# One fp32 layer on one core: weight-sum additions and additions of squares given to GpSimd, other buffers for the low halves of W_O's last product, six low halves no longer stored

## The chip, the cores and the metric

The kernel runs on 1 core of one Trainium2 chip. The metric is the device time of one execution in microseconds. The engines are TensorE (PE in the profile; its weight loads are PEld), VectorE (DVE), ScalarE (ACT), GpSimd (POOL) and SyncE (SP, which here only issues DMAs). GpSimd issues DMAs too, on a queue of its own.

## The reference, cut

One layer over 2112 tokens (2048 of a prompt, 64 of a sample with a state of its own), model width 1024, everything in fp32:

```
h      = rms_norm(x, g_pre);   proj = h @ w_in        # ten projections of 1024 columns
vA, bA, cA, zA, q, f, iv, zB, gA, gB = split(proj)
yA     = (silu(zA) * bA * causal_conv3(cA * vA)) @ w_a_out                  # path A
fg     = lb + (1 - lb) * sigmoid(f)
o      = hgrn2_scan(S0, silu(q) * scale, 1 - fg, iv, log(fg))  # path B: 8 heads, state 128 x 128, chunks of 64
yB     = (rms_norm(o) * silu(zB)) @ w_b_out
out    = (sigmoid(gA) * yA + sigmoid(gB) * yB) @ w_o
x      = x + rms_norm(out, g_post)
gate   = sigmoid(rms_norm(x, g_ple) @ w_ple_gate);    x = x + (p @ w_ple_proj) * gate
```

Results are the new x of both streams, the last columns of the convolution and the states of path B.

## The kernel before

**Numbers.** Activations lie with features on the 128 partitions and tokens along the columns. TensorE multiplies at a rounded form of fp32, so each operand is split into a high half (a cast, ScalarE) and a low half (the operand minus its high half, VectorE, `split`, L196). A product is three matmuls for each slice of 128 features: high x high, high x low, low x high (L380 to L382 in `sgroup`, L514 to L516 in `in_turn`). The third one reads the low half of the weights.

**Tokens.** They are worked through in three blocks of 768, 704 and 640 columns. Each is handled as two halves of 384, 352 and 320 columns.

**Seven products in place of eight.** Weights are taken in pairs of column blocks, which gives 2 x 2 quarters (A11, A12, A21, A22) against two halves of the features and two halves of the tokens. A pair takes seven products, with sums of weight quarters (S1 to S4) and sums of activations (T1 to T4). `sgroup` does the seven products of one pair one after another; the input projections go so. Its first group after W_O (by_k) begins with four products side by side, so it needs the low halves of S3, S1 and S2 at about the same time. `in_turn` does product 1 for four pairs, then product 2 for four pairs, and so on, over the stages W_A, W_B and W_O: 3 x 7 x 4 steps of 12 matmuls. Product 3 uses S2, product 4 S3, product 6 S1, product 7 S4. After each of products 2, 5, 6 and 7 in W_O, the stage's `sink` puts a finished piece of the output into xo (L427 where it is an addition), and `sum_squares` squares it on ScalarE (L635) and adds the square to an accumulator on VectorE (L636). `final_norm` reads that accumulator in the next block's first groups: transposes on TensorE (L616), a reduction on VectorE (L617), a reciprocal root on GpSimd (L576), and then one load of x per row block (L1185, GpSimd's queue).

**Where weight sums come from.** In the first block, the sums for the input projections are made in `combined`. Those for W_A, W_B and W_O are made in `prepare_sums`, 12 pairs of four sums, while path B (7 pairs) and path A (5 pairs) run: GpSimd's queue loads the four quarters (L338), VectorE adds (L361), GpSimd's queue stores the sum (L343), ScalarE and VectorE split it, and GpSimd's queue stores the low half (L347). Later passages, 6 pairs with 24 additions, do the same for groups used in the last block. After that a sum is loaded by SP's queue (`raw<-S`, L206), cast by ScalarE, and its low half is loaded by SP's queue too (L228).

**Buffers for low halves.** A loaded low half gets one of 4 `lo` buffers or one of 3 `s` buffers, by a counter:

```
def low_tile():
    turn[0] += 1
    return sum_tile(F32R) if turn[0] % 7 in (1, 3, 5) else lo_tile()
```

Buffers of a kind are used in rotation, and SP's queue works in order: a load into a buffer whose last reader hasn't finished holds what is queued behind it. Low halves that are made for the first time go into `lo` and are stored for later blocks (L234, SP's queue) if `split_w` was given a key.

**Order.** Engines take their instructions in an order that a list scheduler sets when the kernel is built, with marks in the code that tie side work to places in the stream of matmuls (`hooks`, `behind_all`, `issue_after`). `plain_group` does a pair without sums, with eight products, where the sums are not there yet: it opens the first block.

Of the kernel before, what the change touches and what calls it, by code (L numbers as in the profile page):

```python
# [14 lines left out]
ALU = mybir.AluOpType  # L15
# [17 lines left out]
W_A, W_B, W_O, W_G = 80, 88, 96, 104  # L33
# [55 lines left out]
def hybrid_step(  # L89
# [41 lines left out]
    def wide(x):  # L131
        return x.shape[1]
# [71 lines left out]
    def load_raw(src):  # L204
        raw = wp.tile([P, 4, P], F32, tag="raw", name=nm("raw"), bufs=5)
        SP.dma_start(raw, src)  # L206
        return raw
# [118 lines left out]
    def pairs_of(idx):  # L326
        return [(idx + g, idx + KH + g) for g in range(KH)]

    def prepare_sums(groups):


        def tile_of(dt=F32):
            return rt(4 * P, dt).rearrange("p (k c) -> p k c", c=P)

        def load(i1, i2):
            out = [tile_of() for _ in range(4)]
            for t, (i, h) in zip(out, ((i1, 0), (i2, 0), (i2, 1), (i1, 1))):
                G.dma_start(t, w_blk[i, h])  # L338
            return out

        def keep(name, i1, s):
            sums.setdefault(i1, {})[name] = dram.tile([P, 4, P], F32, tag=f"{name}_{i1}", name=nm(name), bufs=1)
            G.dma_start(sums[i1][name], s)  # L343
            lows[i1, name] = dram.tile([P, 4, P], F32, tag=f"lo{i1, name}", name=nm("low"), bufs=1)
            lo = tile_of(F32R)
            split(s, lo, lo)
            G.dma_start(lows[i1, name], lo.bitcast(F32))  # L347

        nxt = load(*groups[0])
        yield  # L350
        for n, (i1, i2) in enumerate(groups):
            a11, a21, a22, a12 = nxt
            if n + 1 < len(groups):
                nxt = load(*groups[n + 1])
            for name, out, x, y, op in (
                ("S1", a22, a21, a22, ALU.add),
                ("S3", a21, a11, a21, ALU.subtract),
                ("S2", a11, a22, a11, ALU.subtract),
                ("S4", a12, a12, a11, ALU.subtract),
            ):  # L360
                V.tensor_tensor(out, x, y, op)  # L361
                keep(name, i1, out)
                yield

# [46 lines left out]
    def half(t, h):  # L411
        n = wide(t) // 2
        return t[:, h * n : (h + 1) * n]
# [15 lines left out]
    def plain_group(i1, i2, hs, sink, raws=None, between=None):  # L429


        w, ps = {}, {}

        def split_of(c, h):
            key = ((i1, i2)[c], h)
            raw = raws[c, h] if raws else load_raw(w_blk[key])
            with nullcontext() if raws else tc.high_priority():
                w[c, h] = split_w(raw, None if (c, h) == (1, 0) else key)

        for c, h in ((0, 0), (1, 0)) if between else ((0, 0), (0, 1), (1, 0), (1, 1)):  # L440
            with behind_all(() if between else summed[2 + c]):
                split_of(c, h)

        def add(c, ks):
            for k in ks:
                hi, lo = w[c, k // KH]
                for h in range(2):
                    xhi, xlo = hs[k][h]
                    if (c, h) not in ps:
                        ps[c, h] = ps_gemm(wide(xhi))  # L450
                    T.matmul(ps[c, h], hi[:, k % KH, :], xhi, start=k == 0, stop=False)
                    T.matmul(ps[c, h], hi[:, k % KH, :], xlo, start=False, stop=False)
                    last[0] = T.matmul(ps[c, h], lo[:, k % KH, :], xhi, start=False, stop=k == KB - 1).ins

        if between:
            for k in range(KB):
                between()
                for c in range(2):
                    if k == 2:
                        split_of(c, 1)  # L460
                    with placed():
                        add(c, (k,))
        for c in range(2):
            if not between:
                with placed():
                    add(c, range(KB))
            for h in range(2):
                sink(c, h, ps[c, h], None)
# [19 lines left out]
    def in_turn(stages, operand):  # L488


        todo = [(st, n) for st in stages for n in range(7)]
        made = {0: operand}

        def prepare(i, k):
            if i < len(todo):
                st, n = todo[i]
                made.setdefault(i, []).append(operand_of(st["raw"], IN_TURN[n][1], k))

        for i, (st, n) in enumerate(todo):
            if n == 0:  # L500
                st["mid"], st["bank"] = [], {}
            xs = made.pop(i)
            for g in range(KH):
                i1, i2 = st["idx"] + g, st["idx"] + KH + g
                with tc.high_priority():
                    hi, lo = kept_w(i1, i2, IN_TURN[n][0], IN_TURN[n][0] in st["anew"])
                start = n in (0, 2, 3, 5)
                if start:
                    st["bank"][g] = ps_gemm(wide(xs[0][0]))
                ps = st["bank"][g]  # L510
                add = partial(T.matmul, ps, skip_group_check=not start)
                for k in range(KH):
                    xhi, xlo = xs[k]
                    add(hi[:, k, :], xhi, start=start and k == 0, stop=False)  # L514
                    add(hi[:, k, :], xlo, start=False, stop=False)  # L515
                    last[0] = add(lo[:, k, :], xhi, start=False, stop=k == KH - 1).ins  # L516
                if n == 6:
                    prepare(i + 1, g)
                if n == 0:
                    st["mid"].append(rt(2 * wide(ps)))  # L520
                    with tc.high_priority():
                        copies[0] = A.copy(half(st["mid"][g], 0), ps).ins
                u2, p7 = half(st["mid"][g], 0), half(st["mid"][g], 1)
                if n == 1:
                    st["sink"](g, 0, 0, ps, None)
                elif n == 2:
                    adds[0] = V.tensor_tensor(u2, u2, ps, ALU.add).ins
                elif n == 3:
                    with tc.high_priority():
                        copies[0] = A.copy(p7, ps).ins  # L530
                elif n == 4:
                    st["sink"](g, 1, 0, u2, ps)
                elif n == 5:
                    p5 = hf(wide(ps))
                    with tc.high_priority():
                        copies[0] = A.copy(p5, ps).ins
                    adds[0] = V.tensor_tensor(p7, p7, p5, ALU.add).ins
                    st["sink"](g, 1, 1, u2, p7)
                elif n == 6:
                    st["sink"](g, 0, 1, u2, ps)  # L540
                if n < 6:
                    prepare(i + 1, g)
                hook()
                yield st["idx"], n, g
# [82 lines left out]
            copy(out[:, cols_of(sg)], spread(col, sg["n"]))  # L627
        yield

    def sum_squares(j, src, acc, n):  # L630
        if j == 0:
            A.activation(acc, src, AF.Square)
        else:
            sq = hf(n) if n <= MAXN // 2 else rt(n)
            A.activation(sq, src, AF.Square)  # L635
            V.tensor_tensor(acc, acc, sq, ALU.add)  # L636

    def load_x(bl, k):
        t = rt(bl["n"])
# [513 lines left out]
            dict(idx=W_B, raw=ob, sink=sink_b, anew=("A11", "A12")),  # L1153
        ], loads

    def out_in_turn(mg, xo, acc, anew):
        xo.extend([None] * KB)
        begun = set()

        def sink(g, c, h, x, y):  # L1160
            j = g + c * KH
            if not acc:
                acc.append(rt(wide(mg[0])))
            if xo[j] is None:
                xo[j] = rt(wide(mg[0]))
            v = half(xo[j], h)
            into(v, x, y)
            sum_squares(int(h in begun), v, half(acc[0], h), wide(v))
            begun.add(h)

        return dict(idx=W_O, raw=mg, sink=sink, anew=anew)
# [198 lines left out]
    for bi, bl in enumerate(blocks):  # L1370
# [3 lines left out]
        late = [(FF * 8, QQ * 8), (GB * 8 + KB - 2, GB * 8 + KB - 1)]  # L1374
        in_heads = (pairs_of(W_A) + pairs_of(W_B))[:-1] if first else late if middle else None
        in_path = pairs_of(W_B)[-1:] + pairs_of(W_O) if first else pairs_of(W_G) if bl["last"] else None
        extra = prepare_sums(in_heads) if in_heads else None
        path_b(bl, hc, first, kept, fills, hs if first else None, extra, (0, 2) if first else (0,))
        run(fills)
        a = []  # L1380
# [15 lines left out]
        def ready():  # L1396
            a_first.extend(narrow(half(t, 0)) for t in a[:KH])

        path_a(bl, hc, a, first, side(rows, prepare_sums(in_path) if in_path else None), ready)
        assert not hooks and (extra is None or next(extra, extra) is extra)  # L1400
        mg, xo, h2, acc = [], [], [], []
        stages, loads = merge_in_turn(a, kept, mg)
        stages.append(out_in_turn(mg, xo, acc, ("A11", "A12", "A22") if bl["last"] else ()))
        if nxt:
            hc = new_operands()
            ops = operands_in_steps(hc, cols, partial(load_x, nxt), nxt["n"])
# [88 lines left out]
```

## Time and profile before

| | |
|---|---|
| time, median of 3 runs | 2575.61 us (2574.92 to 2575.83) |
| the profiled execution | 2570.03 us, span 2567.7 us, mean granted TensorE clock 0.999 |
| TensorE busy | 2543.4 us, 99% of the span, 16246 matmuls |
| VectorE busy | 1886.0 us, 73% |
| ScalarE busy | 1591.9 us, 62% |
| GpSimd busy | 391.0 us, 15% |
| SP's queue, share of 16 DMA engines | 59.5% (510.59 MB) |
| GpSimd's queue, share of 16 DMA engines | 18.0% (166.25 MB) |

The span is the time from the first to the last recorded instruction of the profiled execution. Busy time is the time in which an engine has at least one instruction at work, without DMA issues. A row of the trace such as `880.17 0.34 PE L516 MATMUL pg<-r,s ...` is one or more instructions: start and length in us, engine, line, operation, output tile `<-` input tiles, shape. What stands in square brackets behind it is how long the engine had been idle before and what ended that wait. `pg` is an accumulator of TensorE in PSUM, `r` a buffer of activations or of `prepare_sums`, `hf` a half-width one, `hi`, `lo` and `s` are the buffers of weights. SPq is SP's DMA queue.

### The profile page before, as it was taken

What the parts mean: (1) busy time and instruction counts of PE and PEld (TensorE: products, weight loads), DVE (VectorE), ACT (ScalarE), POOL (GpSimd) and SP (SyncE); (2) the same over time, 40 slices, a digit from 0 to 9 for tenths busy, and PEclk for the clock granted to TensorE, in tenths of its full rate; (3) what the DMA queues carried; (4) which work ended last, traced back from release to release, by engine and by line L of the source; (5) the groups of instructions that cost most, each with busy time, mean ns of one, the idle gap of its engine ahead of it and who ended that gap; (6) DMA issues with size and microseconds to landing.
All of it is one profiled execution on the core that took longest, in us unless ns stands there. A gap on an engine that the chain in (4) does not pass through costs nothing. (4 is left out here: it accounts for less than half of the span.)

```text
span 2567.7 us, 47073 instructions
## 1 busy us (share of the span) xinstructions
PE 2543.4 (99%) x16246; PEld 2528.9 (98%) x16246; DVE 1886.0 (73%) x3630; ACT 1591.9 (62%) x3076; POOL 391.0 (15%) x718
## 2 busy tenths in 40 slices
PE   8999999999999999999999999999999999999999
PEld 8999999999999999999999999999999999999998
DVE  8788888899989865666665557986566666678966
ACT  6666676554555664577774545676677765566736
POOL 1022121222110021121011101102100011111221
PEclk9999999999999999999999999999999999999999
DMA  7678777898798797676557768989866678899977
GB/s 274 211 262 276 275 251 262 296 318 305 265 324 269 249 341 271 202 241 199 183 180 237 232 212 303 318 279 336 312 199 194 201 240 291 302 309 344 308 263 259
DMA packets 324847, 679.89 MB, mean 265 GB/s; under 512 B 40544, under 2 KB 45184, under 8 KB 324608
## 3 DMA queue, kind: packets, MB, share of 16 engines
q1 hardware_dynamic: 281664, 510.59, 59.5%
q0 software_dynamic: 42656, 166.25, 18.0%
q8 instruction: 128, 2.10, 0.3%
q14 instruction: 111, 0.91, 0.1%
q10 hardware_dynamic: 288, 0.05, 0.0%
HBM read 496.61 MB, written 180.11 MB: 264 GB/s over the span
## 5 line engine op out<-in xcount | busy, mean ns | idle before, releaser
L380 PE MATMUL pg<-r,hi 128*128 128x320 f32 (+2 forms) x3304 | 1088.6, 329 | 0.0
L381 PE MATMUL pg<-r,hi 128*128 128x320 f32 (+2 forms) x3304 | 1067.7, 323 | 0.0
L382 PE MATMUL pg<-r,lo 128*128 128x384 f32 (+2 forms) x2368 | 772.0, 326 | 1.2 <-DMA lo<-low 1.2
L381 PEld LDWEIGHTS pg<-r,hi 128*128 128x128 f32 x3304 | 623.3, 189 | 0.0
L380 PEld LDWEIGHTS pg<-r,hi 128*128 128x128 f32 x3304 | 622.6, 188 | 0.4
L227 ACT CAST hi<-raw 128x512 fp32r<-128x512 f32 x528 | 325.7, 619 | 337.7 <-PE pg L381 154.1
L196 ACT CAST hi<-raw 128x512 fp32r<-128x512 f32 x458 | 283.4, 620 | 309.4 <-PE pg L381 137.9
L382 PEld LDWEIGHTS pg<-r,lo 128*128 128x128 f32 x2368 | 445.4, 188 | 1.6 <-DMA lo<-low 1.4
L196 DVE TENSOR_TENSOR lo<-raw,hi 128x512 fp32r<-128x512 f32 x458 | 315.4, 690 | 168.2 <-ACT hi L196 127.2
L515 PE MATMUL pg<-r,hi 128*128 128x320 f32 (+2 forms) x1120 | 360.8, 324 | 1.1 <-DVE r L196 0.8
L514 PE MATMUL pg<-r,hi 128*128 128x320 f32 (+2 forms) x1120 | 354.5, 324 | 1.1 <-ACT r L196 1.1
L382 PE MATMUL pg<-r,s 128*128 128x320 f32 (+1 forms) x936 | 296.6, 317 | 3.4 <-DMA s<-low 3.4
L196 DVE TENSOR_TENSOR r<-r,r 128x320 fp32r<-128x320 f32 (+7 forms) x394 | 230.8, 604 | 63.7 <-ACT r L196 62.3
L516 PE MATMUL pg<-r,lo 128*128 128x320 f32 (+2 forms) x776 | 249.8, 323 | 5.0 <-DMA lo<-low 5.0
L196 ACT CAST r<-r 128x320 fp32r<-128x320 f32 (+7 forms) x394 | 205.9, 552 | 16.7 <-DVE r L361 5.6
L515 PEld LDWEIGHTS pg<-r,hi 128*128 128x128 f32 x1120 | 210.6, 188 | 5.0 <-DVE r L196 4.2
L514 PEld LDWEIGHTS pg<-r,hi 128*128 128x128 f32 x1120 | 208.4, 188 | 4.9 <-ACT r L196 4.5
L382 PEld LDWEIGHTS pg<-r,s 128*128 128x128 f32 x936 | 176.8, 189 | 4.0 <-DMA s<-low 4.0
L196 ACT CAST hi<-s 128x512 fp32r<-128x512 f32 x160 | 98.7, 618 | 118.8 <-PE pg L381 103.4
L394 ACT COPY hf<-pg 128x352 f32<-128x352 f32 (+2 forms) x354 | 155.9, 443 | 8.9 <-PE pg L382 8.7
L516 PEld LDWEIGHTS pg<-r,lo 128*128 128x128 f32 x776 | 145.8, 188 | 6.3 <-DMA lo<-low 6.2
L196 DVE TENSOR_TENSOR lo<-s,hi 128x512 fp32r<-128x512 f32 x160 | 110.3, 689 | 36.7 <-PE pg L382 12.8
(367 smaller groups left out, 3846.7 us busy)
## 6 DMA issues: line engine op xcount, KB each, us to landing
raw<-w_blk SPq DMA_DIRECT2D x554, 256.0 KB, 3.9
raw<-S SPq DMA_DIRECT2D x472, 256.0 KB, 3.7
s<-low SPq DMA_DIRECT2D x327, 256.0 KB, 3.9
lo<-low SPq DMA_DIRECT2D x201, 256.0 KB, 4.3
low<-lo SPq DMA_DIRECT2D x194, 256.0 KB, 3.0
S<-s SPq DMA_DIRECT2D x152, 256.0 KB, 3.1
r<-w_blk POOLq DMA_DIRECT2D x72, 256.0 KB, 6.5
S<-r POOLq DMA_DIRECT2D x72, 256.0 KB, 3.4
```

Source lines behind the costliest of these rows:

```text
L196: return A.copy(hi, src).ins, V.tensor_tensor(lo, src, hi.bitcast(F32), ALU.subtract).ins
L227: A.copy(hi, raw)
L380: add(hi[:, k, :], xhi, start=start and k == 0, stop=False)
L381: add(hi[:, k, :], xlo, start=False, stop=False)
L382: last[0] = add(lo[:, k, :], xhi, start=False, stop=k == KH - 1).ins
L394: copied = A.copy(got[n], ps[bank])
L514: add(hi[:, k, :], xhi, start=start and k == 0, stop=False)
L515: add(hi[:, k, :], xlo, start=False, stop=False)
L516: last[0] = add(lo[:, k, :], xhi, start=False, stop=k == KH - 1).ins
```

## The change

1. `prepare_sums` takes the engine of its additions as an argument: GpSimd in the first block (48 additions of 128 x 512), VectorE in the two later passages (24).
2. `sum_squares` takes the engine of its addition: GpSimd for W_O of the first two blocks (14 additions of 128 x 384, 14 of 128 x 352), VectorE everywhere else.
3. Ahead of product 7 of W_O, in each block, the counter of `low_tile` is set to 3. The four low halves of that product then go into `lo, s, lo, lo`.
4. `plain_group` no longer gives `split_w` a key: six low halves fewer are stored by SP's queue in the first block.

```diff
-    def prepare_sums(groups):
+    def prepare_sums(groups, E):
...
-                V.tensor_tensor(out, x, y, op)
+                E.tensor_tensor(out, x, y, op)
                 keep(name, i1, out)
...
         def split_of(c, h):
-            key = ((i1, i2)[c], h)
-            raw = raws[c, h] if raws else load_raw(w_blk[key])
+            raw = raws[c, h] if raws else load_raw(w_blk[(i1, i2)[c], h])
             with nullcontext() if raws else tc.high_priority():
-                w[c, h] = split_w(raw, None if (c, h) == (1, 0) else key)
+                w[c, h] = split_w(raw)
...
             xs = made.pop(i)
+            if (st["idx"], n) == (W_O, 6):
+                turn[0] = 3
...
-    def sum_squares(j, src, acc, n):
+    def sum_squares(j, src, acc, n, E=V):
...
-            V.tensor_tensor(acc, acc, sq, ALU.add)
+            E.tensor_tensor(acc, acc, sq, ALU.add)
...
-    def out_in_turn(mg, xo, acc, anew):
+    def out_in_turn(mg, xo, acc, anew, E):
...
-            sum_squares(int(h in begun), v, half(acc[0], h), wide(v))
+            sum_squares(int(h in begun), v, half(acc[0], h), wide(v), E)
...
-        extra = prepare_sums(in_heads) if in_heads else None
+        extra = prepare_sums(in_heads, G if first else V) if in_heads else None
...
-        path_a(bl, hc, a, first, side(rows, prepare_sums(in_path) if in_path else None), ready)
+        path_a(bl, hc, a, first, side(rows, prepare_sums(in_path, G if first else V) if in_path else None), ready)
...
-        stages.append(out_in_turn(mg, xo, acc, ("A11", "A12", "A22") if bl["last"] else ()))
+        stages.append(out_in_turn(mg, xo, acc, ("A11", "A12", "A22") if bl["last"] else (), V if bl["last"] else G))
```

Two places of the order that the scheduler now sets. The first is SP's queue at the end of W_O in the first block. `raw<-S` loads a full sum, `s<-low` a stored low half into an `s` buffer, `low<-lo` stores a low half; loads into `lo` stand on lines of their own elsewhere. Before, the first row belongs to product 6, pair 3, the next two `s` rows to product 7, pairs 1 and 3:

```order
L228 DMA s_10952<-low_7887 128x512
L206 DMA raw_10920<-S_1882_7452 128x512
L234 DMA low_10783<-lo_10780 128x512
L228 DMA s_11010<-low_7272 128x512
L206 DMA raw_10949<-S_1981_7885 128x512
L234 DMA low_10811<-lo_10808 128x512
L206 DMA raw_10978<-S_2113_8378 128x512
L234 DMA low_10839<-lo_10836 128x512
L206 DMA raw_11007<-S_1833_7270 128x512
L206 DMA raw_11030<-S_1972_7812 128x512
L228 DMA s_11056<-low_8247 128x512
```

After:

```order
L228 DMA s_10940<-low_7875 128x512
L206 DMA raw_10908<-S_1876_7440 128x512
L234 DMA low_10771<-lo_10768 128x512
L228 DMA s_11021<-low_7802 128x512
L206 DMA raw_10937<-S_1975_7873 128x512
L234 DMA low_10799<-lo_10796 128x512
L206 DMA raw_10966<-S_2107_8366 128x512
L234 DMA low_10827<-lo_10824 128x512
L206 DMA raw_10995<-S_1827_7258 128x512
L234 DMA low_10855<-lo_10852 128x512
L206 DMA raw_11018<-S_1966_7800 128x512
L228 DMA s_11117<-low_1591 128x512
```

Now the second `s` row is product 7, pair 2, and the last one is already the next block's first gates (S3): of product 7 only one low half is in an `s` buffer.

The second place is GpSimd's queue at the end of W_O in the first block. The loads of `x_fm` at L640 (L641 after) are the next block's x, those at L1185 (L1186) the norm's x. Before:

```order
L640 DMA r_10281<-x_fm 128x704
L640 DMA r_10283<-x_fm 128x704
L640 DMA r_10916<-x_fm 128x704
L640 DMA r_10918<-x_fm 128x704
L1185 DMA r_11221<-x_fm 128x768
L1185 DMA r_11223<-x_fm 128x768
L1185 DMA r_11225<-x_fm 128x768
L1185 DMA r_11227<-x_fm 128x768
L576 TENSOR_TENSOR colsum_11229<-colsum_11229,mhalf 128x6
```

After:

```order
L637 TENSOR_TENSOR r_10449<-r_10449,hf_10843 128x384
L641 DMA r_10904<-x_fm 128x704
L637 TENSOR_TENSOR r_10449<-r_10449,hf_10871 128x384
L641 DMA r_10906<-x_fm 128x704
L637 TENSOR_TENSOR r_10449<-r_10449,hf_10931 128x384
L637 TENSOR_TENSOR r_10449<-r_10449,hf_10960 128x384
L637 TENSOR_TENSOR r_10449<-r_10449,hf_10989 128x384
L637 TENSOR_TENSOR r_10449<-r_10449,hf_11014 128x384
L637 TENSOR_TENSOR r_10449<-r_10449,hf_11037 128x384
L637 TENSOR_TENSOR r_10449<-r_10449,hf_11060 128x384
L637 TENSOR_TENSOR r_10449<-r_10449,hf_11089 128x384
L1186 DMA r_11209<-x_fm 128x768
```

Nine additions of squares now stand ahead of the norm's first load of x, two of them ahead of or between the last two loads of the next block's x.

## The prediction

> **What bounds the kernel now.** I read the page's engine lines first, then TensorE's waits, then the timeline around the longest of them. The page's line gives share and count of busy time:
>
> ```profile
> PE 2543.4 (99%) x16246; PEld 2528.9 (98%) x16246; DVE 1886.0 (73%) x3630; ACT 1591.9 (62%) x3076; POOL 391.0 (15%) x718
> ```
>
> TensorE is busy all but 24.3 of 2567.7 us, and the change leaves its matmuls as they are. So it can only win back waits, or add some. These are all of TensorE's waits (total, number, longest):
>
> ```profile
> PE pa L1095 <- ACT r L196: 6.9, 1, 6.9
> PE pg L516 <- DMA lo<-low: 5.0, 4, 2.5
> PE pg L382 <- DMA s<-low: 3.4, 2, 2.2
> PE pg L382 <- DMA lo<-low: 1.2, 1, 1.2
> PE pg L514 <- ACT r L196: 1.1, 1, 1.1
> PE pg L515 <- DVE r L196: 0.8, 2, 0.7
> ```
>
> The 6.9 is the start, before any work has arrived. Of the other 11.5 us, 9.6 are low halves that come late by DMA, 1.1 ScalarE's, 0.8 VectorE's. Only two waits stand where the change moves a buffer: the 3.4 on `s<-low`, one at each passage from W_O to the next block's first gates. The first of them (SP's lines are DMA issues; start, length):
>
> ```profile
> 880.17 0.34 PE L516 MATMUL pg<-r,s 128*128 128x384 f32 x1
> ...
> 884.04 0.33 PE L381 MATMUL pg<-r,hi 128*128 128x352 f32 x1
> 886.53 0.43 PE L382 MATMUL pg<-r,s 128*128 128x352 f32 x1 [2.16 <-DMA s<-low]
> ```
> ```profile
> 876.35 0.33 SPq L228 DMA_DIRECT2D s<-low  x1
> 877.10 0.33 SPq L206 DMA_DIRECT2D raw<-S  x1
> 879.31 0.33 SPq L206 DMA_DIRECT2D raw<-w_blk  x1
> 880.53 0.34 SPq L228 DMA_DIRECT2D s<-low  x1
> ```
>
> The load at 880.53 starts as the last matmul that reads an `s` buffer ends (880.17 + 0.34 = 880.51): W_O's product 7, pair 3. It fills the freed buffer with S2's low half for the first gates, due at 884.04 + 0.16 = 884.20, and it lands 6.0 us after its issue. And for a while after this wait TensorE runs slowly (third number from the right is the granted clock):
>
> ```profile
> 887.40:890.90 3.50, 3.50 (x15) 3.50 (x14) 0.78 (x1) 0.00 (x0) 0.00 (x0) 0.52 0.28 109
> 891.20:894.70 3.50, 3.50 (x26) 3.47 (x25) 0.99 (x2) 1.93 (x5) 0.00 (x0) 1.00 0.12 14
> ```
>
> At clock 0.52 these 3.5 us lose 3.5 x 0.48 = 1.7. The second passage has the same wait without a slow stretch:
>
> ```profile
> 1725.66 0.32 SPq L228 DMA_DIRECT2D s<-low  x1
> ...
> 1730.46 0.42 PE L382 MATMUL pg<-r,s 128*128 128x320 f32 x1 [1.27 <-DMA s<-low]
> ```
>
> **The change, part by part.**
>
> *Buffers of W_O's last products.* With the counter at 3, product 7 takes `lo, s, lo, lo` where both first blocks had `s, lo, s, lo`. The last reader of an `s` buffer is pair 2, one pair earlier. A pair is 12 matmuls. A window without a wait (each column here and above: busy time and count of TensorE, its weight loads, VectorE, ScalarE, GpSimd, then clock, DMA share, GB/s) gives their rate:
>
> ```profile
> 513.50:577.70 64.20, 64.20 (x368) 64.20 (x367) 60.29 (x108) 37.98 (x83) 18.24 (x33) 1.00 0.91 318
> ```
>
> 64.2 / 368 = 0.174 us at 384 columns, so 2.1 a pair; at 352 columns 0.160, so 1.9. The third `s` load can go at 880.53 - 2.1 = 878.4, since of the transfers ahead of it on SP's queue only the sum's raw tile (877.10) remains; the raw tile of 879.31 now stands behind it. It lands at 886.5 - 2.1 = 884.4: 0.2 late instead of 2.16 (about 2.3 against an unbroken stream). Gain 2.1; between 0, if another wait on SP's queue holds it, and 2.3. In the second passage it lands 1.9 earlier and the whole 1.27 goes; between 0 and 1.4. The third `lo` of product 7 reuses a buffer of product 6, pair 2, free some 8 us before its use: nothing. The slow stretch I take to follow from the wait, with no other gap of TensorE near it: gain 1.7; between 0 and 1.7.
>
> [...]
>
> *Weight sums on GpSimd.* 48 of the 72 adds at L361 leave VectorE, and 28 of the 70 at L636. Their rows, and the nearest ones on POOL:
>
> ```profile
> L361 DVE TENSOR_TENSOR r<-r,r 128x512 f32<-128x512 f32 x72 | 49.4, 687 | 0.2
> L636 DVE TENSOR_TENSOR r<-r,hf 128x384 f32<-128x384 f32 x14 | 7.8, 559 | 1.4 <-ACT hf L635 1.3
> L636 DVE TENSOR_TENSOR r<-r,hf 128x352 f32<-128x352 f32 x14 | 7.3, 523 | 0.6 <-ACT hf L635 0.6
> L870 POOL MEMSET hf<- 128x64 f32 x8 | 1.4, 170 | 0.0
> ```
>
> VectorE sheds 48 x 0.69 + 14 x 0.56 + 14 x 0.52 = 48 us. No row has an add on POOL. Below, it is bounded by VectorE's 0.69 for 512 columns; above by the memset, 170 / 64 = 2.7 ns a column for one stream, 1.36 us for 512, 4.1 for an add's three streams. I take 1.4, twice VectorE's row, because the operation and shape are that row's; 1.1 at 384, 1.0 at 352. POOL gains 48 x 1.4 + 14 x 1.1 + 14 x 1.0 = 97 us (48 to 250) on 391 busy: it stays idle most of the time. On its queue the add now comes ahead of the store of the same sum (L343), where it waited for VectorE anyway, so that the store is not later; the squareroot steps (L576) stand behind the same stores of low halves as before. Sums are read first in W_A, far later. In all that time, 64 to 702 us, TensorE waits for nothing, so the relief is worth nothing; and the cover for a mishap is VectorE's idle time, least in the window of 513.50 above and the two behind it (VectorE is the third pair):
>
> ```profile
> 577.70:641.90 64.20, 64.20 (x368) 64.20 (x367) 59.11 (x100) 30.79 (x58) 15.14 (x29) 1.00 0.88 305
> 641.90:706.10 64.20, 64.20 (x370) 64.16 (x369) 58.50 (x99) 33.81 (x65) 10.30 (x20) 1.00 0.80 265
> ```
>
> 14.7 us idle in 192.6; the 19 adds there take 13 us out of VectorE's load. Cost 0.
>
> *Squares in W_O.* The 28 adds at L636 sit in W_O of blocks 1 and 2, one per pair of products 2, 5, 6 and 7. Behind them on POOL's queue now stand loads of the next block's x (L640) and of the norm's x (L1185):
>
> ```profile
> 864.91 1.07 POOL L640 DMA_DIRECT2D r<-x_fm  x2 [57.96 <-PE pg L516]
> 878.50 0.54 POOL L1185 DMA_DIRECT2D r<-x_fm  x1 [12.52 <-DVE r L427]
> ```
>
> The second L640 goes after the add of product 5, pair 4, some 3 us later; VectorE takes up that tile at 878.1, 9 us after. L1185 goes behind the last add, at 887, and is added first after the norm's scale, past 898. The sum of squares itself ends about as before:
>
> ```profile
> 886.03 0.55 DVE L636 TENSOR_TENSOR r<-r,hf 128x384 f32<-128x384 f32 x1
> 886.50 1.69 DVE L196 TENSOR_TENSOR r<-r,r 128x704 fp32r<-128x704 f32 x2
> 894.14 0.82 PE L616 MATMUL pa<-ident,r 128*128 128x128 f32 x6
> ```
>
> The gates start at 882.4 (880.17 + 13 x 0.174: one pair is left). TensorE's transposes come 48 matmuls of 0.160 later, 7.7 us: at 890.1 without the wait. The last product's addition stands at 883.77, its square 0.55 + 0.5 later, an add of 1.1 ends at 886: hidden by 4 us. VectorE, without a gap from 874 to 888, drops seven of these adds, 3.3 us, so that the splits of 886.50 come earlier; TensorE does not wait for them. Gain 0, of at most the 0.8 in the list.
>
> *Fewer low halves stored.* Six stores of 256 KB in the first 60 to 100 us go from SP's queue, each 0.4 us of issue. TensorE waits for no load there. Nothing.
>
> Sum: 2.1 + 1.7 + 1.3 = 5.1 us. The profiled execution took 2570.03, its span 2567.7: 2570.03 - 5.1 = 2564.9. The median of the runs shown lies 5.6 above that execution (2575.61), and the same step gives 2570.5.
>
> **Rivals.**
>
> [...]
>
> 2. *GpSimd's adds hold VectorE up*, so that the relief turns round. At the end of W_O seven adds of 1.1 cost 7.7 against 3.3 saved; the second split of 886.50 (T2's last operand, done at 887.4) moves to 891.8, due at 882.4 + 45 x 0.160 = 889.6: TensorE waits 2. With 1 at the second passage: gain 2, 2573.5. Against it: a two-input addition of VectorE ran its usual 0.69 us wholly inside an operation of POOL that reads SBUF:
> ```profile
> 131.22 1.04 POOL L576 TENSOR_TENSOR ms<-ms,mhalf 128x4 f32<-128x4 f32 x1 [63.40 <-DVE ms L574]
> 131.50 0.69 DVE L314 TENSOR_TENSOR s<-raw,raw 128x512 f32<-128x512 f32 x1
> ```
> That one reads only four columns, though. [...]
>
> 3. *Slower: the squares come too late for the norm.* If an add takes 3.1 us (the upper bound, 4.1 x 384/512), eleven of them from 866 end at 900, 10 us behind the transposes at 890.1, and TensorE stands, here and (2.8 each, about 8) at the second passage: 18 - 5 = 13 slower, 2588. It decides from 2.2 us an add, (890.1 - 866) / 11. Against it: that takes four times VectorE's duration.
>
> 4. *The low halves of W_O and W_A land otherwise*: `s` and `lo` alternate differently from there on, and SP's order is a new one, so that the 5.0 us of waits at L516 may grow or shrink by 3 to 5: 2565 or 2575.
>
> **How the numbers follow.** 0.2% of the median, 5.15 us, is about what a measurement can tell from no change, and my sum lies on that edge. The forecast, 2570.5 (own range 2568 to 2573), has chance 0.50, half of it beyond the edge on the fast side, with some weight for the small terms that I put at 0: 0.30. Rival 1 has 0.13, of it 0.03 faster; rival 2 has 0.15, of it 0.03 slower (VectorE filling up between 513 and 706 too, from 1.4 + 0.1 us per add on: 14.7 idle + 13 saved, over 19); rival 3 has 0.07, all slower; rival 4 has 0.15, of it 0.08 faster and 0.03 slower. Faster 0.41, same 0.46, slower 0.13. The range, 2563 to 2580, leaves out rival 3 and the tails of 2 and 4.
>
> **What would show it.** Right: no wait on `s<-low` above 0.5 us at either passage, the `s` load issued about 2 us earlier against the gates' first matmul, clock 1.00 through the first gates; adds at L361 on POOL of 1 to 1.5 us with VectorE's rows unchanged (0.69, 0.56). Wrong: VectorE's two-input rows grown or idle beside POOL's adds; TensorE waiting at L382 for VectorE's splits or at the transposes of L616 for POOL; new waits on `lo<-low` elsewhere.

## The result, and the profile after

The changed kernel is slower. In the first comparison its undisturbed runs took 2587.63 and 2591.89 us; ratio to before 1.0058, 95% interval 1.0038 to 1.0077 (the median on record, 3061.67 us, is that of four runs of which two, 3531 and 5407 us, were disturbed). Timed again beside other kernels it took 2584.98 us against 2572.99; ratio 1.0053 (1.0040 to 1.0066). That is some 12 to 15 us more, where 5 less were forecast.

The profiled execution has a span of 2585.9 us, 18.2 more than before. The page's line of busy times, and then TensorE's waits (total, number, longest):

```profile
PE 2550.4 (99%) x16246; PEld 2532.2 (98%) x16246; DVE 1905.5 (74%) x3554; ACT 1586.3 (61%) x3076; POOL 493.4 (19%) x794
```
```profile
PE pg L382 <- DMA lo<-low: 8.1, 3, 5.6
PE pa L1096 <- ACT r L196: 7.1, 1, 7.1
PE pg L517 <- DMA lo<-low: 3.7, 2, 2.5
PE pa L1038 <- DVE r L1033: 3.2, 5, 1.3
PE pg L380 <- DVE r L427: 3.1, 4, 1.1
PE pg L516 <- DVE r L196: 2.5, 4, 0.8
```

VectorE has 76 instructions fewer and is busy 19.5 us longer. The wait on `s<-low` is gone, as forecast. New are waits for VectorE (L1038, L380, L516) and a much longer one on `lo<-low` at L382. TensorE's busy time itself is 7.0 us longer, in part by stretches of half clock behind the longer waits (mean granted clock 0.997 against 0.999).

TensorE executes the same number of matmuls in both kernels, so the n-th matmul's start can be compared between the two traces. The lag of the changed kernel grows by 7.3 us between 174 and 646 us (path B and A of the first block, where the weight sums are made), falls by 3.1 at the first passage from W_O to the gates and 0.9 at the second, and grows by 3.5 at 936 us and by 6.0 at 1760 us, behind the passages.

**Where VectorE lost.** GpSimd's additions took about what was forecast: 1.36 us for 1.4, and in W_O 1.31 and 1.09 for 1.1 and 1.0 (busy, mean ns, idle before):

```profile
L361 POOL TENSOR_TENSOR r<-r,r 128x512 f32<-128x512 f32 x48 | 65.3, 1360 | 42.8 <-DMA r<-w_blk 42.1
L637 POOL TENSOR_TENSOR r<-r,hf 128x384 f32<-128x384 f32 x14 | 18.3, 1310 | 63.1 <-ACT hf L636 62.2 <-DVE r L196 0.6
L637 POOL TENSOR_TENSOR r<-r,hf 128x352 f32<-128x352 f32 x14 | 15.3, 1094 | 58.5 <-ACT hf L636 57.8 <-DVE r L196 0.5
```

But VectorE's instructions with two operands in SBUF did not run beside them. One stretch of the timeline, GpSimd, VectorE and the wait of TensorE that follows (start, length):

```profile
511.34 1.54 POOL L361 TENSOR_TENSOR r<-r,r 128x512 f32<-128x512 f32 x1 [7.43 <-DMA r<-w_blk]
513.77 1.31 POOL L361 TENSOR_TENSOR r<-r,r 128x512 f32<-128x512 f32 x1
515.98 1.31 POOL L361 TENSOR_TENSOR r<-r,r 128x512 f32<-128x512 f32 x1
```
```profile
511.65 1.78 DVE L196 TENSOR_TENSOR lo<-s,hi 128x512 fp32r<-128x512 f32 x1
513.47 2.17 DVE L314 TENSOR_TENSOR s<-raw,s 128x512 f32<-128x512 f32 x1
515.56 2.29 DVE L196 TENSOR_TENSOR lo<-s,hi 128x512 fp32r<-128x512 f32 x1
517.77 0.54 DVE L427 TENSOR_TENSOR r<-hf,pg 128x384 f32<-128x384 f32 x1
```
```profile
518.46 0.41 PE L380 MATMUL pg<-r,hi 128*128 128x384 f32 x1 [0.95 <-DVE r L427]
```

The same four instructions before:

```profile
505.32 0.69 DVE L196 TENSOR_TENSOR lo<-s,hi 128x512 fp32r<-128x512 f32 x1
506.05 0.69 DVE L314 TENSOR_TENSOR s<-raw,s 128x512 f32<-128x512 f32 x1
506.65 0.69 DVE L196 TENSOR_TENSOR lo<-s,hi 128x512 fp32r<-128x512 f32 x1
507.26 0.55 DVE L427 TENSOR_TENSOR r<-hf,pg 128x384 f32<-128x384 f32 x1
```

Each of the three with both operands in SBUF ends 0.55 or 0.56 us after the addition of GpSimd that it meets, so most of its usual 0.69 us lies behind GpSimd's addition. That holds for the second and third too, although the profile has them start 0.30 and 0.42 us ahead of the addition. The fourth, whose second operand lies in PSUM (`pg`), takes its usual time but stands behind the others, and its reader on TensorE waits 0.95 us.

In path B the wait comes later, at the end of a chain. Here VectorE grows by 3.8 us in four instructions that meet additions, against 0.69 us each for the first three and 0.55 for the last:

```profile
262.61 1.53 DVE L196 TENSOR_TENSOR lo<-raw,hi 128x512 fp32r<-128x512 f32 x1 [0.16 <-PE pg L382]
265.87 0.99 DVE L196 TENSOR_TENSOR lo<-s,hi 128x512 fp32r<-128x512 f32 x1
267.04 2.01 DVE L314 TENSOR_TENSOR s<-raw,s 128x512 f32<-128x512 f32 x1
269.23 1.86 DVE L427 TENSOR_TENSOR r<-hf,hf 128x384 f32<-128x384 f32 x1
```
```profile
273.86 0.52 ACT L852 ACTIVATE r<-hf 128x384 f32<-128x384 f32 x1 [3.09 <-DVE hf L420]
284.96 0.41 PE L1038 MATMUL pa<-ident,r 128*128 128x128 f32 x2 [1.34 <-DVE r L1033]
```

ScalarE gets `hf` late and so squares path B's output late (L1030). Behind the squares come VectorE's reduction, the reciprocal root on GpSimd, VectorE's multiplication (L1033) and TensorE's transposes, which wait 1.34 us.

Over the whole trace, some 90 two-operand instructions of VectorE (TENSOR_TENSOR) on SBUF met an addition of GpSimd; measured against the median of their own group they grew by 62.7 us, with 77.4 us spent side by side. 17 with a PSUM operand met one and did not grow (below 0.1 us in all, with 6.2 us spent side by side). So VectorE shed 48 us and was charged 63. The groups show it, the third row being the one with PSUM:

```profile
L314 DVE TENSOR_TENSOR s<-raw,s 128x512 f32<-128x512 f32 x40 | 36.5, 914 | 0.3
L427 DVE TENSOR_TENSOR r<-hf,hf 128x384 f32<-128x384 f32 x38 | 28.1, 741 | 0.2
L427 DVE TENSOR_TENSOR r<-hf,pg 128x384 f32<-128x384 f32 x38 | 20.7, 546 | 0.0
```

Before, these rows had means of 687, 554 and 548 ns.

**Where the low halves came late.** The norm's first four loads of x went one by one from 878.50 to 881.58 before, ahead of the gates' start (882.44). Now they stand behind the last addition of squares on GpSimd's queue and go together, 6.4 and 6.2 us after the gates' starts (892.85 and 1739.25):

```profile
899.28 2.19 POOL L1186 DMA_DIRECT2D r<-x_fm  x4
...
1745.46 2.15 POOL L1186 DMA_DIRECT2D r<-x_fm  x4
```

Then TensorE waits for low halves of weights; the last row is a load for the first of these waits, and it landed 10.2 us after its issue, where 4.4 is the median of its kind:

```profile
936.14 0.43 PE L382 MATMUL pg<-r,lo 128*128 128x352 f32 x1 [1.98 <-DMA lo<-low]
...
1760.17 0.64 PE L382 MATMUL pg<-r,lo 128*128 128x320 f32 x1 [5.63 <-DMA lo<-low]
```
```profile
925.89 0.98 SPq L228 DMA_DIRECT2D lo<-low  x1
```

### The profile page after: what moved, and what is told of

It is laid out like the page before. It is cut to its first block, busy times and chain, and to the rows that moved or that the text cites. A ratio compares the mean times of both kernels' runs of the same rounds, so it can differ in the third digit from the quotient of the medians.

```text
span 2585.9 us, 47049 instructions
## 1 busy us (share of the span) xinstructions
PE 2550.4 (99%) x16246; PEld 2532.2 (98%) x16246; DVE 1905.5 (74%) x3554; ACT 1586.3 (61%) x3076; POOL 493.4 (19%) x794
## 5 line engine op out<-in xcount | busy, mean ns | idle before, releaser
L380 PE MATMUL pg<-r,hi 128*128 128x320 f32 (+2 forms) x3304 | 1087.3, 329 | 3.1 <-DVE r L427 3.1
L382 PE MATMUL pg<-r,lo 128*128 128x384 f32 (+2 forms) x2368 | 772.0, 326 | 8.1 <-DMA lo<-low 8.1
L380 PEld LDWEIGHTS pg<-r,hi 128*128 128x128 f32 x3304 | 622.7, 188 | 4.9 <-issue 3.6
L382 PEld LDWEIGHTS pg<-r,lo 128*128 128x128 f32 x2368 | 445.8, 188 | 9.5 <-DMA lo<-low 8.9
L196 DVE TENSOR_TENSOR lo<-raw,hi 128x512 fp32r<-128x512 f32 x458 | 327.0, 715 | 159.4 <-ACT hi L196 116.3
L516 PE MATMUL pg<-r,hi 128*128 128x320 f32 (+2 forms) x1120 | 362.0, 324 | 2.8 <-DVE r L196 2.5
L382 PE MATMUL pg<-r,s 128*128 128x320 f32 (+1 forms) x936 | 296.0, 316 | 0.0
L516 PEld LDWEIGHTS pg<-r,hi 128*128 128x128 f32 x1120 | 210.8, 188 | 7.8 <-DVE r L196 6.9
L382 PEld LDWEIGHTS pg<-r,s 128*128 128x128 f32 x936 | 176.1, 188 | 0.0
```

Of the source, the lines that this page charges most:

```text
L196: return A.copy(hi, src).ins, V.tensor_tensor(lo, src, hi.bitcast(F32), ALU.subtract).ins
```

## The experiments

All ratios are to the kernel before on the same chip, with 95% intervals. "Faster" and "slower" mean an interval that leaves out 1.

**Part 3 alone: buffers of W_O's last product.**

```diff
             xs = made.pop(i)
+            if (st["idx"], n) == (W_O, 6):
+                turn[0] = 3
```

> The kernel before with part 3 alone (counter set to 3 ahead of W_O's last product); all additions on VectorE. Theory A (the loss of 16 us comes from GpSimd's additions: they stop VectorE's two-operand instructions, and they push the norm's loads of x into the next block's first gates): the step at the two passages from W_O to the gates stays as in the changed kernel, 3.1 and 0.9 us won, and the late low halves 45 us (then 1.98 us of wait) and 20 us (5.63 us) behind the passages do not come: 4 us faster, ratio 0.998. Theory B (the new alternation of the two buffer kinds and the new order of SP's queue make those late low halves): they come here too, 3.5 + 6.0 - 4.0 = 5 us slower, ratio 1.002.

2568.57 us against 2574.36; ratio 0.9974 (0.9964 to 0.9984): faster. The third `s` load of the first passage goes at 878.52 (880.53 before), and no wait on `s<-low` is left among TensorE's waits:

```profile
878.52 0.33 SPq L228 DMA_DIRECT2D s<-low  x1
```
```profile
PE pg L518 <- DMA lo<-low: 4.9, 4, 2.8
PE pg L516 <- ACT r L196: 2.0, 1, 2.0
PE pg L382 <- DMA lo<-low: 1.7, 1, 1.7
PE pg L517 <- DVE r L196: 0.7, 1, 0.7
```

TensorE gains 4.0 us at the first passage and 1.5 at the second. Theory B falls: the new alternation of the buffers makes no new late low halves.

**Part 1 alone: weight sums on GpSimd in the first block** (`E.tensor_tensor(out, x, y, op)` with `E` as in the change).

> The kernel before with part 1 alone (48 additions of weight sums on GpSimd in the first block). Theory A: TensorE's stream falls back by the 7.3 us that the changed kernel lost between 174 and 646 us, with waits for VectorE at the transposes of path B and at L380, and VectorE's two-operand rows with both operands in SBUF grow by about as long as they lie beside an addition, some 45 us in all: 5 to 8 us slower, ratio 1.003. Theory B: the additions are only slow themselves, VectorE is relieved, and the 7.3 us come from the order: no change, within 2 us.

2580.63 us against 2574.36, 6.3 more; ratio 1.0028 (1.0019 to 1.0037). The waits for VectorE in path B are there (L1037: 4.0 us, 6 times), VectorE's instructions grew by 47.4 us beside the 48 additions (52.0 us side by side). In that trace VectorE's rows had grown by 3.4 to 4.3 us in the 27 us ahead of each of these six waits. So theory B falls. The wait on `s<-low` at the first passage grew too, by which TensorE loses another 1.9 us:

```profile
PE pg L382 <- DMA s<-low: 5.5, 2, 4.0
PE pa L1037 <- DVE r L1032: 4.0, 6, 1.4
```

**Part 2 alone: squares of W_O on GpSimd** (`E.tensor_tensor(acc, acc, sq, ALU.add)` with `E` as in the change).

> The kernel before with part 2 alone (28 additions of squares on GpSimd in W_O of the first two blocks). Theory A: the waits for s<-low at the two passages stay (2.2 and 1.3 us), the norm's first four loads of x go some 20 us later against the gates' start, behind the last addition, and low halves come late in the first gates: 3.5 us more behind the first passage, 6 behind the second, 5 to 10 us slower, ratio 1.003. Theory B: the loads of x are hidden as before, within 2 us of the kernel before.

2578.51 us, 4.2 more; ratio 1.0015 (1.0006 to 1.0024). The low halves come late behind both passages (2.8 and 4.9 us of wait). One thing was expected wrongly: the waits for `s<-low` are gone here too, without the change of buffers. The third `s` load landed 3.0 us after its issue, where it took 6.0 before, beside the loads of x. That wait had two parents, the late issue and the loads of x beside it, and either cure removes it. Hence the gain of part 3 and this one may not be added. VectorE's instructions grew by 13.7 us beside these 28 additions, about the 15 us that they take off it: VectorE's time comes out even there, unlike with the weight sums.

**Parts 3 and 4 alone: the changed kernel with all additions on VectorE.**

> The changed kernel with every addition back on VectorE: parts 3 and 4 alone (buffers, fewer stores). Theory A: as with part 3 alone, 4 to 5 us faster than before, ratio 0.998, and some 18 us faster than the changed kernel. Theory B: slower than before by 3 to 8 us, since the order of buffers and of SP's queue is the changed kernel's.

2566.28 us against 2574.36; ratio 0.9971 (0.9961 to 0.9982). This version beats both kernels. Its interval overlaps that of part 3 alone: the six stores are worth nothing that can be told.

**The changed kernel again.**

> The changed kernel, unchanged, timed again beside the others, since only two undisturbed runs of it stand so far (2587.6 and 2591.9 us). The parts alone came to -6 (buffers), +6 (weight sums) and +4 us (squares), 4 us in all, but the gain of the buffers and of the later loads of x in the kernel with the squares is the same wait, counted twice: the parts together would give 4 + 4 = 8 us slower, ratio 1.003. If it comes out at 1.005 or more, the additions also make each other's waits worse.

2584.98 us against 2572.99, 12.0 more; ratio 1.0053. Above the expected 8. Weight sums (6.3) and late loads of x (6.0, next run, in which the `s<-low` gain is contained) make 12.3; with part 2's own 4.2 they make 10.5. The interval (1.0040 to 1.0066) is some 10 to 17 us, so whether the additions also make each other's waits worse, as was expected for 1.005 or more, is not shown. The profiled execution has the long wait behind the second passage (5.0 us at 1756) but none near 936: how late the low halves come behind the first passage differs between executions.

**Late loads of x, with all additions on VectorE.**

```diff
-                G.dma_start(xks[j][:, c], ...)
+                d = G.dma_start(xks[j][:, c], ...)
+                if not bl["last"] and j < 4:
+                    paced(d)
```

> The kernel before, all additions on VectorE; only the first four loads of x of each of the two norms after W_O are held until a matmul of the next block's first gates (their 48th, 7.7 us after the gates' start; in the kernel with the squares on GpSimd they go 6 to 7 us after it). Theory A1 (these late loads alone make the late low halves 45 and 20 us behind the passages, by filling the DMA engines): low halves late again by 2 and 5 us there, and no wait for s<-low at the passage itself, as with the squares on GpSimd: 3 to 6 us slower, ratio 1.002. Theory A2 (VectorE, held up by the additions of squares, frees the raw buffers late, and the loads of weights bunch): no late low halves, the waits for s<-low gone, 3 to 4 us faster, ratio 0.9985.

2578.99 us, 6.0 more; ratio 1.0024 (1.0012 to 1.0036). No addition runs on GpSimd here, and the low halves come late all the same, 2.94 us at 929 and 7.99 at 1753:

```profile
894.09 2.12 POOL L1185 DMA_DIRECT2D r<-x_fm  x4 [24.63 <-PE pg L382]
```
```profile
PE pg L382 <- DMA lo<-low: 10.9, 2, 8.0
```

So A1 stands: the time of these eight loads alone does it. A2, which put it down to VectorE, falls.

**The changed kernel with early loads of x.** A list `xks` of four tiles is filled in the loop over `in_turn` and handed to `final_norm`:

```diff
             if nxt:
+                if (idx, n, g) == (W_O, 6, 0):
+                    first_x(bl, xks)
                 continue
```

> The changed kernel; only the first four loads of x of these two norms are asked for after product 7's first pair, so that on GpSimd's queue they stand ahead of the last seven additions of squares. Theory A1: the waits for low halves of 2.0 us (at 936) and 5.6 us (at 1760) and the slow clock behind each go, 8 to 10 us faster than the changed kernel, about 2580 us, ratio to before 1.002. Theory A2: they stay, since the additions stand where they stood: as the changed kernel, within 3 us.

2578.79 us, 6.2 less than the changed kernel in the same series; ratio to before 1.0026 (1.0013 to 1.0038). The waits for `lo<-low` at L382 shrink from 8.1 us to 1.0:

```profile
PE pg L517 <- DMA lo<-low: 7.3, 6, 2.7
...
PE pa L1038 <- DVE r L1033: 3.0, 5, 0.9
...
PE pg L382 <- DMA lo<-low: 1.0, 2, 0.5
```

So theory A1 holds for the waits. Less came back in time than expected. The 5.8 us that stay are not the weight sums alone: the new buffers should have taken off some 4 to 6 us. By the starts of the matmuls, TensorE falls back by 5.3 us between 174 and 646 us, wins 3.1 at the first passage and 0.1 at the second (a wait on `s<-low` of 0.6 us stands there), and falls back by another 5.4 between 2280 and 2420 us, in the last block, where the first trace of the changed kernel lost 1.6. In W_A to W_O there are more waits for low halves than in the first trace of the changed kernel (7.3 against 3.7 us), which I have not followed up.

**Loads of the next block's x held back.** `STEPS_AT` has 28 in place of the first 20, and the second pair of loads at L641 is `paced`; else as the version with parts 3 and 4.

> Buffers and fewer stores as in the run without GpSimd's additions; besides, the second pair of loads of the next block's x (734.6 us in the kernel before, 10 us ahead of the wait of 2.5 us for a low half at 745, DMA share 1.04) is asked for 8 steps later and held until a matmul there (about 761 us, DMA share 0.8). Theory A1 in general (loads of x on full DMA engines delay low halves): the wait at 745 (2.5 us before, 3.2 in that run) shrinks below 1 us and the slow clock behind it with it, 3 to 5 us faster than that run, ratio to before 0.9955. If the stores of low halves alone fill the engines there: as that run, 0.997.

2566.08 us against 2572.99; ratio 0.9978 (0.9969 to 0.9986). The wait at 745 shrinks from 3.2 us (in that run) to 1.3 and no slow clock follows, but the time can't be told from that version's 0.9971. Without the loads of x the DMA share from 734 to 744 us is still 1.04, so the loads made a good half of that wait in these two traces. No gain was shown.

**GpSimd's work by itself.** VectorE keeps its additions; behind each of the 48, GpSimd works once more on the sum, in place, first with two operands, then with one:

```diff
                 V.tensor_tensor(out, x, y, op)
+                if more:
+                    flat = out.rearrange("p k c -> p (k c)")
+                    G.tensor_tensor(flat, flat, ones.to_broadcast([P, 4 * P]), ALU.mult)
```
```diff
+                if more:
+                    G.tensor_copy(out, out)
```

> The kernel before, additions on VectorE; behind each of the 48 weight-sum additions of the first block GpSimd multiplies the sum by one, in place, 128x512 with two operands (the second is one column, read again and again). Theory A (a two-operand operation of GpSimd stops VectorE's two-operand operations on SBUF): VectorE isn't relieved of anything here and is stopped by about as long as before, 40 to 50 us in all, so that TensorE loses at least the 6 us of the run with the sums on GpSimd: 6 to 15 us slower, ratio 1.004. Theory C (what cost 6 us there is the longer chain of load, addition and store on GpSimd, not VectorE): 0 to 2 us, VectorE's rows as before.

> As the run with the multiplications, but GpSimd copies each of the 48 sums in place (one operand, 128x512). Theory A in its narrow form (only two operands on GpSimd stop VectorE): VectorE's rows as in the kernel before, within 2 us, ratio 1.000. In its wide form (any work of GpSimd in SBUF stops VectorE): as with the multiplications, VectorE's rows longer by the length of the copies that they meet, 4 to 15 us slower.

```profile
L364 POOL TENSOR_TENSOR r<-r,ones 128x512 f32<-128x512 f32 x48 | 65.4, 1363 | 116.3 <-DVE r L361 111.5 <-DVE cols L577 4.4
```
```profile
L363 POOL COPY r<-r 128x512 f32<-128x512 f32 x48 | 47.6, 991 | 119.3 <-DVE r L361 114.8 <-DVE cols L576 4.4
```

The multiplications: ratio 1.0016 (1.0006 to 1.0027), VectorE's TENSOR_TENSOR on SBUF grew by 28.2 us in 53.0 side by side. So VectorE was stopped although it was relieved of nothing, and theory C, which left its rows as before, falls as written. But the time grew by about 4 us and not the 6 to 15 expected, and at another place: TensorE loses nothing between 64 and 646 us here, and 6.0 us near 710 us, in W_A (waits of 1.2 us for VectorE and 1.5 for ScalarE, then half clock), where the copies' trace loses 2.2 too. So these runs do not price the 6.3 us of the sums; that rests on the waits of part 1's trace. The copies: ratio 0.9993 (0.9984 to 1.0003), VectorE grew by 10.3 us in 37.9 side by side. Neither form of theory A holds as written: one operand stopped VectorE too, about half as much for each us side by side (10.3 / 37.9 = 0.27 against 28.2 / 53.0 = 0.53), and this much cost no time that can be told. GpSimd was held up as well: its shortest and median times are 0.61 and 1.00 us for the copies, 1.05 and 1.41 for the multiplications, and 1.28 and 1.30 for the additions of the changed kernel. So here the two engines share the loss, and beside the additions VectorE bears nearly all of it.

## Why the prediction was wrong

- **Buffers of W_O's last products: right.** Forecast 5.1 us, of it 3.8 and 1.3 at the passages, and the forecast mechanism is what came: part 3 alone gave 5.8 by the medians, 4.0 and 1.5 in the trace. The load went at 878.52 for a forecast 878.4, and the slow stretch went with the wait, so rival 1, by which it stays (2572.2), is out. What I did not see is that the wait depended on the loads of x beside it as well: with these late, TensorE wins there without the new buffers too (3.0 us in part 2 alone, 4.0 with the late loads alone).
- **Weight sums, "Cost 0": the step that failed first.** The duration was right (1.36 us for a forecast 1.4). I let them run beside VectorE, since one pow of GpSimd over 4 columns had left a VectorE instruction at 0.69 us. That row said nothing of an addition over 512 columns. With the sums alone, a relief of 33 us (48 x 0.69) came with a charge of 47 us. That TensorE waited for nothing between 64 and 702 us was no cover: VectorE's slack, 15 us in 193, was counted together with 13 us of relief, and the chain through path B had less. Measured: 6.3 us, of it 1.9 at the first passage by the trace.
- **Squares, "Gain 0": the second failed step.** I saw that L1185 goes behind the last add and asked only when its data are used (late enough: rival 3 did not occur, the waits at the transposes are absent). I did not ask what the loads meet when they go later. The row of 891.20 that I quoted for its clock (DMA share 0.12) shows the DMA engines nearly idle in the first gates, and the next stretch of that trace (first row) shows them full; so does the changed kernel's (second and third), where the loads go at 899.28, with the rush instead of ahead of it:

```profile
895.00:900.00 5.00, 5.00 (x35) 4.97 (x34) 3.01 (x7) 4.17 (x7) 2.12 (x2) 1.00 1.02 357
```
```profile
895.00:900.00 5.00, 4.87 (x30) 4.90 (x31) 5.00 (x6) 2.85 (x5) 3.41 (x4) 1.00 0.05 11
900.00:905.00 5.00, 5.00 (x35) 4.98 (x34) 3.86 (x9) 4.13 (x9) 2.51 (x4) 1.00 1.00 360
```

Measured by the loads alone: 6.0 us, with the wait on `s<-low` that they no longer cause already deducted.
- **Fewer stores: nothing, right.**
- **Rivals.** Rival 2 was the mechanism, but with its price at the wrong place: at the end of W_O I gave it 2 to 3 us (TensorE waited 0.7 us for VectorE there), and filling VectorE between 513 and 706 us got 0.03. The growth went by where the operands lie: 62.7 us of growth with both in SBUF against less than 0.1 with one in PSUM. Starting first did not spare VectorE: 34 instructions of VectorE that started ahead of an addition of weight sums, by the profile, grew by 30.5 us in 31.5 side by side. Rival 4 is out by the run with part 3 alone: waits of 4.9 us for low halves at that line, for 5.0 before.
- **Slips in the sums.** The upper bound of GpSimd's load is 279 us by its own terms, not 250; 18 additions start in the three windows, not 19; the second split at 886.50 ends at 888.2, not 887.4, so that rival 2's wait of 2 would be nearer 3. None of them moves the forecast.

Summed: 6.3 for the sums and 6.0 for the late loads give 12.3, and 12.0 were measured; the gain of part 3 is inside the second number. That it fits to 0.3 us is luck: each interval is 2 to 3 us wide to either side, and the 1.9 us at the first passage are in the first number but not in the changed kernel, which has no wait on `s<-low`.

## What to carry to other kernels

Before an addition goes from VectorE to GpSimd, look at what VectorE runs meanwhile: with two operands in SBUF it stood still here for most of GpSimd's longer time (1.36 against 0.69 us; 62.7 us of growth in 77.4 side by side). The 48 weight sums alone cost VectorE 47 us for 33 saved, the 28 squares alone 14 for 15. The 17 instructions with an operand in PSUM that met an addition did not grow (below 0.1 us in all). An instruction that is put into a queue that also issues DMAs can move the DMAs behind it: here the additions of squares moved the norm's first load of x from 3.9 us ahead of the first gates' start to 6.4 us after it. Such a load is to be priced by the DMA share at its new time as well as by when its data are due. Two gains that cure the same wait are counted once.

## What the runs showed of the hardware

In these traces it depended on where a wait of TensorE fell whether a slow stretch followed it. The stretches of half clock ahead of the kernel's end last 3.41 us, or two or three times that. The first row is the one behind the wait at 936 us; the second is the latter half of one from 1756.8 to 1763.6 us, whose former half lies in the wait itself (the clock is the third number from the right):

```profile
937.60:941.00 3.40, 3.40 (x14) 3.40 (x13) 2.08 (x3) 2.18 (x4) 0.54 (x1) 0.50 1.03 410
1760.10:1763.50 3.40, 3.33 (x12) 3.33 (x13) 1.05 (x2) 0.52 (x1) 0.55 (x1) 0.50 0.92 303
```

In the changed kernel's trace they end at 756.7, 941.0 and 1763.6 us: 184.3 and 822.6 us apart, which is 54.0 and 241.0 times 3.413; the first two last 3.413 us each by the trace's clock records. So take the time in windows of that length, counted from where an execution's half clock starts. Eleven profiled executions have slow stretches ahead of their end. In them, from the start of the clock records on (10.3 and 12.6 us in the traces before and after), each window at full clock in which TensorE was idle for 0.57 of it or more (20 windows) was followed by one at half clock, and none idle for 0.53 or less was, with one exception (0.40, two waits of 1.2 and 1.5 us close together, in the run with the multiplications). In the traces before and after, half clock followed the windows at full clock idle for 0.63 (before) and for 0.67, 0.57 and 0.66 (after), and full clock those idle for 0.50 or less. So the wait of 2.53 us at 745 in the kernel before, which fell on two windows (0.50 and 0.24), cost no clock, and one of 2.16 us at 886 did (0.63). The rows of the first of the two, the wait and the 3.5 us behind it:

```profile
744.98 0.44 PE L516 MATMUL pg<-r,lo 128*128 128x384 f32 x1 [2.53 <-DMA lo<-low]
744.90:748.40 3.50, 3.42 (x20) 3.42 (x21) 0.48 (x2) 1.41 (x3) 0.54 (x1) 1.00 0.92 311
```

That is an analysis of traces; no run was made to vary where a wait falls.
